# One decoder layer on one Trainium2 core: expert chunks, gathers and the last rows placed at other points of the program

## The chip, the cores and the metric

The kernel runs on one core of one Trainium2 chip. The metric is device time in microseconds (us) of one execution. The engines of the core are PE (TensorE: matmuls, with PEld its weight loads), DVE (VectorE), ACT (ScalarE), POOL (GpSimd) and SP (SyncE, used here only to issue DMAs). Each engine runs its instructions in the order in which they stand in its own stream; DMAs are issued by SP, ACT and POOL and move data on 16 shared DMA engines.

## The reference, cut to what matters

The layer has 512 tokens of width 1024. First comes a mixer; then, on the result x2, a retrieval layer (PEER) with 16384 experts:

```
x = x + merged @ W_out                       # attention and a gated recurrence, merged
h = rms_norm(x, norm_ffn_g)
q = (h @ w_q).reshape(B, S, 8, 2, 128)       # 8 heads, two half keys
sc = einsum('bshpd,phnd->bshpn', q, keys)    # 128 scores for each half key
v1, i1 = top_k(sc[..., 0, :], 16); v2, i2 = top_k(sc[..., 1, :], 16)
best, pos = top_k(v1 + v2 (all pairs), 16);  idx = i1 * 128 + i2 at pos
gates = softmax(best)
act = gelu(einsum('tkd,td->tk', u[idx], h))
x = x + einsum('tk,tkd->td', gates * act, v[idx])
return rms_norm(x, norm_final_g)
```

u and v have 16384 rows of 1024 float32 each. Every token uses 8 x 16 = 128 experts.

## The kernel before

Float32 operands of a matmul are split into a high part (`hi`, made on ACT at line 142) and a rest (`lo`, made on DVE at line 162, or 145), and three products are summed.

**Front** (lines 182 to 615): first RMS norm, projections, recurrence, attention, merge, x2, second norm. `tokens` (213 to 225) loads a piece of x transposed and scales it by `gm`, the first norm's scale vector, which line 275 loads through POOL's queue. `proj_tm` and `proj_fm` are the projections (lines 255 to 265).

**The expert layer is done in two ways.** Tokens 160 to 511 (DT = 352) are treated densely: expert row i2 = 0..127 is a *chunk* c. The U part of a chunk (`act_pieces`, line 638) loads 512 KB of u, splits it, makes 24 matmuls of 352 columns (line 646) and applies gelu; the result is a `gel` tile. The V part (lines 973 to 996) loads 512 KB of v, multiplies the gel tile with the chunk's gate weights G, and adds into six PSUM banks `acc` with 18 matmuls of 512 columns (lines 994 to 996). Tokens 0 to 159 (block 0 and 32 more) are treated by gathers: `gather` (704) has POOL fetch 128 rows of u or v by an indirect DMA into one of GB = 4 buffers, and `sparse` (711) uses them on DVE (line 715 for u, 725 for v). There are NS = 320 such steps: 160 for u, then 160 for v. `pace(goal, after)` (729) issues gathers up to a goal, and three gathers behind each one the DVE step, which is kept behind the instruction `after` on DVE.

**Routing** (lines 828 to 870): for 16 half keys hp a projection (24 matmuls of 512 columns), scores (line 847), top 16 of 128 on DVE (854 to 858), and per head the choice of 16 pairs (`route`, 752). `fill(n)` puts n whole U chunks between; here `int(F1*(hp+1)) - int(F1*hp)` per half key, which is 24 in all.

**G stage** (lines 876 to 917): after two more U chunks, the gates of the 352 tokens become dense matrices. For each 8 tokens DVE makes four one-hot tiles (904 to 907, two buffers `oh`), PE makes 8 small matmuls for each 4 tokens (912), ACT copies them out (914), and each 16 tokens are written to memory (`Gd`, 22 writes of 1 MB on ACT's queue). After each 4 tokens `piece` puts in a quarter of a U chunk, 88 quarters, so 22 chunks. Up to seven gathers are issued here.

**Transition** (938 to 945): three U chunks, loads of v, the load of the first G part (`g_load(0)`, which waits for the last write of Gd), gathers up to EARLY = 16, and two more U chunks, whose loads stand behind that of G on SP's queue.

**Loop** (973 to 1021) over the 128 chunks: V part of chunk c; until c = 115 the 75 U chunks that are left; `pace` by a share of the work done. **End** (1000 to 1029): at c = 120 x2 is loaded again; at c = 122 the 32 tokens' rows are finished; after the loop come the last gather steps, the rows of block 0 and those of `acc` (`final_rows`, 955: add, square, sum, scale, write).

KEEP = 53 gel tiles are live at once: 26 (LOOK) in a pool of their own, 17 (LATE) in `gel2`, which takes the memory that routing frees, and 10 in `extra`.

The order of each engine's stream is made by a planner with costs of its own from the order of the program; `tc.issue_after(x)` keeps an instruction behind x on x's engine, `keep_in_program_order` keeps it where it was written.

Of the kernel before, what the change touches and what calls it, by code (L numbers as in the profile page):

```python
# [6 lines left out]
F32 = mybir.dt.float32  # L7
# [5 lines left out]
OP = mybir.AluOpType  # L13
# [4 lines left out]
P = 128  # L18
# [8 lines left out]
NE = 128  # L27
# [4 lines left out]
DT = S - T0  # L32
# [14 lines left out]
VPRE = 2  # L47
GLAG = 3
GB = 4
TAILC = 2  # L50
HELD = 5
LASTU = 2
EARLY = 16
UEND = 116
TL = 2
F1 = 1.5


def host(inp):
# [57 lines left out]
def layer(nc, tc, a, out, probe=None, upto=99):  # L117
# [9 lines left out]
    def nm(s):  # L127
        uid[0] += 1
        return f"{s}_{uid[0]}"
# [25 lines left out]
    def wsplit(raw, shape, parts=1, eng=None):  # L155
        hi = oc.tile(list(shape), F32R, tag="hi", bufs=HB, name=nm("hi"))
        lo = oc.tile(list(shape), F32R, tag="lo", bufs=HB, name=nm("lo"))
        n = shape[1] // parts
        for i in range(parts):
            m = slice(i * n, (i + 1) * n)  # L160
            hi_of(hi[:, m], raw[:, m])
            (eng or V).tensor_tensor(lo[:, m], raw[:, m], hi[:, m].bitcast(F32), op=OP.subtract)  # L162
        return hi, lo


# [26 lines left out]
    with tc.tile_pool(name="front", bufs=1) as fr, tc.tile_pool(name="psf", bufs=1, space=PSUM) as psf:  # L192
# [79 lines left out]


        ktm, logf = [], []
        POOL.dma_start(gm, a["gmix"])
        POOL.dma_start(ones, a["const"][:, 5 * P:6 * P])
        ld = exp_ln_set()
        fb = proj_tm(0)
# [342 lines left out]
    with tc.tile_pool(name="peer", bufs=1) as pp, tc.tile_pool(name="psp", bufs=1, space=PSUM) as psp, ExitStack() as ps:  # L621
# [7 lines left out]
        def gel_tile(c):  # L629
            i = c % KEEP  # L630
            if i < LOOK:
                return pp.tile([P, DT], F32, tag="gel", bufs=LOOK, name=nm("gel"))
            if i < LOOK + LATE:
                return cur["gel2"].tile([P, DT], F32, tag="gel2", bufs=LATE, name=nm("gel"))
            return extra[i - LOOK - LATE]


        def act_pieces(c, pin=False):
# [33 lines left out]
        def piece(limit):  # L672
            while len(work) < 2 and nu[0] < limit:
                work.append(act_pieces(next(todo), True))
                next(work[-1])
                nu[0] += 1
            if work and next(work[0], 0) == 0:
                work.pop(0)
# [197 lines left out]
        with tc.tile_pool(name="gb", bufs=1, reuse_waits="tile") as gp:  # L876
            iT = gp.tile([P, 2, DT], F16, name="iT")
            gs = gp.tile([P, DT], F32, name="gs")
            g16 = gp.tile([P, 2, DT], F16, name="g16")
            fill(2)  # L880
            for n in range(1, NB):
                f = X if n == 1 else 0
                t = slice((n - 1) * P - X + f, n * P - X)
                b = bank((P, 4, P))
                for w in range(2):
                    PE.transpose(b[:, w, :], i12[:, w, n, :], ident)
                PE.transpose(b[:, 2, :], gta[:, n, :], ident)
                ACT.activation(iT[:, :, t], b[:, 0:2, f:], AF.Copy)
                ACT.activation(gs[:, t], b[:, 2, f:], AF.Copy, scale=GS)  # L889
                V.tensor_copy(g16[:, 0, t], gs[:, t])  # L890
                V.tensor_tensor(g16[:, 1, t], gs[:, t], g16[:, 0, t], op=OP.subtract)
            NQ = OT // QT
            shape = [P, NQ, P, QT]
            for s_ in range(NPT):
                G_ = gp.tile([P, NE, TG], F32, tag="G", bufs=2, name=nm("G"))
                for o in range(TG // OT):
                    t = slice(s_ * TG + o * OT, s_ * TG + (o + 1) * OT)

                    def row(x):
                        return x.rearrange("p (q t) -> p q t", t=QT).unsqueeze(2).to_broadcast(shape)  # L900

                    ioq = iok.unsqueeze(1).to_broadcast(shape)
                    oh = gp.tile([P, 3, NQ, P, QT], F16, tag="oh", bufs=2, name=nm("oh"))
                    V.tensor_tensor(oh[:, 0], ioq, row(iT[:, 0, t]), op=OP.is_equal)
                    V.tensor_tensor(oh[:, 2], ioq, row(iT[:, 1, t]), op=OP.is_equal)
                    V.tensor_tensor(oh[:, 1], oh[:, 2], row(g16[:, 0, t]), op=OP.mult)
                    last = V.tensor_tensor(oh[:, 2], oh[:, 2], row(g16[:, 1, t]), op=OP.mult)
                    for q in range(NQ):
                        b = bank((P, QT, P))
                        for i in range(QT):  # L910
                            for w in range(2):
                                lastg = tc.keep_in_program_order(PE.matmul(b[:, i, :], oh[:, 0, q, :, i], oh[:, 1 + w, q, :, i], start=w == 0, stop=w == 1))  # L912
                        m = o * OT + q * QT
                        ACT.activation(G_[:, :, m:m + QT].rearrange("p c t -> p t c"), b, AF.Copy)
                        piece(KEEP - HELD)
                ACT.dma_start(Gd.rearrange("g p s f -> s p g f")[s_], G_.rearrange("p (g c) t -> p g (c t)", c=GC))
                pace((s_ + 1) // 3, last.ins)
        late = ps.enter_context(tc.tile_pool(name="late", bufs=1, reuse_waits="tile"))
# [17 lines left out]
                return SP.dma_start(gts[g], Gd[g])  # L936

        with tc.issue_after(lastg.ins):
            fill(KEEP - nu[0] - LASTU)
        for c in range(VPRE):  # L940
            v_load(c)
        g0 = g_load(0)
        pace(EARLY, last.ins)
        with tc.issue_after(lastg.ins), tc.issue_after(g0.ins):
            fill(LASTU)

# [22 lines left out]

        todo_u = NE - nu[0]  # L970
        nu0 = nu[0]
        ready = []
        for c in range(NE):
            if c % GC == 0:
                g_load(c // GC + 1)
            gtile = gts[c // GC][:, :, (c % GC) * TG:(c % GC + 1) * TG]
            v_load(c + VPRE)
            vh, vl = wsplit(vraw.pop(c), [P, D])
            w = late.tile([P, DT], F32, tag="w", bufs=2, name=nm("w"))
            V.scalar_tensor_tensor(w.rearrange("p (s t) -> p s t", t=TG), gel.pop(c).rearrange("p (s t) -> p s t", t=TG),  # L980
                                   1.0 / GS, gtile, op0=OP.mult, op1=OP.mult)
            whi = late.tile([P, DT], F32R, tag="whi", bufs=2, name=nm("whi"))
            hi_of(whi, w)
            wlo = late.tile([P, DT], F32R, tag="wlo", bufs=2, name=nm("wlo"))
            last = V.tensor_tensor(wlo, w, whi.bitcast(F32), op=OP.subtract)  # L985
            ready.append((c, whi, wlo, vh, vl))
            if c < NE - TL or c == NE - 1:
                for tb in range(DB):
                    t = slice(tb * P, min(tb * P + P, DT))
                    m = t.stop - t.start  # L990
                    for i, whi, wlo, vh, vl in ready:
                        for hf in range(2):
                            d = slice(hf * 512, (hf + 1) * 512)
                            PE.matmul(acc[tb][hf][0:m, :], whi[:, t], vh[:, d], start=i == 0, stop=False)  # L994
                            PE.matmul(acc[tb][hf][0:m, :], whi[:, t], vl[:, d], start=False, stop=False)  # L995
                            PE.matmul(acc[tb][hf][0:m, :], wlo[:, t], vh[:, d], start=False, stop=i == NE - 1)  # L996
                ready = []
            fill(min(NE, nu0 + -(-todo_u * (c + 1) // UEND)) - nu[0])
            share = (c + 1 + nu[0] - nu0) / (NE - TAILC + todo_u)
            if c == NE - 8:  # L1000
                ld = exp_ln_set()
                yt = [e8([P, 2, D]) for _ in range(2)]
                ys = [yt[n // 2][:, n % 2, :] for n in range(NB)]
                gf = h20
                SP.dma_start(gf, a["gfin"].to_broadcast([P, D]))
                xf = xs_.rearrange("n p d -> (n p) d")
                yx = s4([P, D])
                SP.dma_start(yx[0:X, :], xf[P:T0])
                for n in range(NB):
                    t = T0 + (n - 1) * P if n else 0  # L1010
                    m = min(P, S - t)
                    SP.dma_start(ys[n][0:m, :], xf[t:t + m])
            if c == NE - 6:

                assert nsp[0] >= NS - sp0.w
                bs = []
                for hf in range(2):
                    bs.append(bank(tag="p"))
                    PE.matmul(bs[hf][0:X, :], fold[:, 0:X], sp1.ax[:, hf * 512:(hf + 1) * 512], start=True, stop=True)
                final_rows(yx[0:X, :], [b[0:X, :] for b in bs], P, X)  # L1020
            pace(EARLY + (NS - EARLY) * share, last.ins)

        while nsp[0] < NS:
            sparse(nsp[0])
            nsp[0] += 1
        final_rows(ys[0], [sp0.ax[:, 0:512], sp0.ax[:, 512:]], 0, P)
        for n in range(DB):
            m = min(P, DT - n * P)
            final_rows(ys[n + 1][0:m, :], [acc[n][hf][0:m, :] for hf in range(2)], T0 + n * P, m)
# [17 lines left out]
```

## Time and profile before

| | |
|---|---|
| Three runs | 1669.36, 1670.48, 1662.62 us; median 1669.36 |
| Profiled execution | 1675.46 us, its span 1673.7 us |
| Mean granted TensorE clock | 0.986 |
| PE busy | 1605.2 us (96%) |
| DVE busy | 1321.9 us (79%) |
| ACT busy | 709.6 us (42%) |
| POOL busy | 487.3 us (29%) |
| HBM traffic | 371.91 MB read, 27.39 MB written |

The profiled execution was the slowest of the four. Busy time of PE counts a matmul from its start to its modelled end; consecutive matmuls overlap, so 96% does not say that PE had no room. What PE can do is read from the spacing of matmuls that follow one another.

### The profile page before, as it was taken

The numbers are of one execution on the slowest core, as the hardware profiler recorded it, in microseconds if no ns is written. First come the engines' busy times: TensorE is split into PE (matmuls) and PEld (weight loads), VectorE is DVE, ScalarE is ACT, GpSimd is POOL, SyncE is SP. The second block draws the span as 40 slices with busy tenths as digits, with TensorE's granted clock in tenths as the row PEclk, the third lists the DMA queues.
The fourth block names the chain that finished last, engine by engine and source line by source line (L and its number), as shares of the span: only waits on it lengthen the run. The fifth ranks groups of instructions, "written<-read, shape, count | busy, mean of one in ns | idle before, by whom it ended". The sixth has DMA issues, their size and how long they took to land.

```text
span 1673.7 us, 23435 instructions
## 1 busy us (share of the span) xinstructions
PE 1605.2 (96%) x8511; PEld 1358.7 (81%) x8511; DVE 1321.9 (79%) x2560; ACT 709.6 (42%) x1152; POOL 487.3 (29%) x341
## 2 busy tenths in 40 slices
PE   8999999999999969997899999999999999999996
PEld 6877678888988869997788888887888888888874
DVE  8456663647999988887688888878888888888887
ACT  5433353234554547775333333333333333333333
POOL 4000000000000010002455555445455555554542
PEclk9999999999999979999899999999999999999998
DMA  5311133334333347888999999999999999999984
GB/s 173 101 51 51 51 104 111 103 115 154 108 109 116 103 126 192 219 224 265 336 340 353 349 368 349 337 341 339 344 368 351 359 354 347 360 358 363 343 305 145
DMA packets 197491, 400.87 MB, mean 240 GB/s; under 512 B 103344, under 2 KB 105904, under 8 KB 197376
## 3 DMA queue, kind: packets, MB, share of 16 engines
q1 hardware_dynamic: 58832, 206.02, 35.2%
q0 software_dynamic: 46336, 168.39, 27.0%
q10 hardware_dynamic: 92208, 24.98, 6.1%
q8 instruction: 66, 1.08, 0.3%
q14 instruction: 49, 0.40, 0.1%
HBM read 371.91 MB, written 27.39 MB: 239 GB/s over the span
## 4 chain that ended last, share of the span: by engine, by line
PE 53%; issue 16%; POOL 12%; DVE 12%; DMA 6%; ACT 1%; POOLq 0%; DVEq 0%; SPq 0%; ACTq 0%
PE b L646 13%; POOL ga L707 11%; PE b L263 5%; PE b L262 5%; PE b L995 5%; PE b L996 5%; PE b L265 4%; PE b L994 4%; DMA ga<-v,idx 4%; PE b L912 4%; DVE lo L162 3%; DMA ga<-un,idx 1%; DVE ti L858 1%; DVE mr L856 1%; DVE e L725 1%
## 5 line engine op out<-in xcount | busy, mean ns | idle before, releaser
L707 POOL DMA_INDIRECT ga<-un,idx x160 | 225.2, 1407 | 944.5 <-ACT gs L889 581.3
L646 PE MATMUL b<-hT,hi 128*128 128x352 f32 x2048 | 366.9, 327 | 2.2 <-ACT hi L142 1.7
L646 PEld LDWEIGHTS b<-hT,hi 128*128 128x128 f32 x2048 | 334.4, 190 | 12.7 <-ACT hi L142 2.0
L995 PE MATMUL b<-lo,whi 128*128 128x512 f32 (+1 forms) x768 | 305.0, 397 | 15.0 <-DVE lo L162 14.6
L996 PE MATMUL b<-hi,wlo 128*128 128x512 f32 (+1 forms) x768 | 304.3, 396 | 0.0
L994 PE MATMUL b<-hi,whi 128*128 128x512 f32 (+1 forms) x768 | 302.7, 395 | 0.0
L707 POOL DMA_INDIRECT ga<-v,idx x160 | 240.4, 1502 | 208.3 <-DVE e L725 190.3
L142 ACT ACTIVATE hi<-s 128x1024 fp32r<-128x1024 f32 (+1 forms) x195 | 205.1, 1052 | 203.1 <-PE b L646 88.1
L162 DVE TENSOR_TENSOR lo<-s,hi 128x1024 fp32r<-128x1024 f32 (+1 forms) x195 | 238.5, 1224 | 29.7 <-ACT hi L142 28.0
L142 ACT ACTIVATE whi<-w 128x352 fp32r<-128x352 f32 x128 | 63.7, 498 | 400.0 <-PE b L995 361.2
L725 DVE SCALAR_TENSOR_TENSOR e<-ga,wt,e 128x1024 f32<-128x1024 f32 x158 | 202.2, 1280 | 19.3 <-DMA ga<-v,idx 18.4
L715 DVE SCALAR_TENSOR_TENSOR ga<-ga,h 128x1024 f32<-128x1024 f32 x160 | 194.5, 1220 | 28.6 <-DMA ga<-un,idx 26.9
L646 PE MATMUL b<-hT,lo 128*128 128x352 f32 x1024 | 191.3, 325 | 11.8 <-DVE lo L162 11.8
L995 PEld LDWEIGHTS b<-lo,whi 128*128 128x128 f32 (+1 forms) x768 | 138.8, 181 | 59.2 <-DVE lo L162 22.0
L646 PEld LDWEIGHTS b<-hT,lo 128*128 128x128 f32 x1024 | 168.0, 189 | 12.4 <-DVE lo L162 12.3
L996 PEld LDWEIGHTS b<-hi,wlo 128*128 128x128 f32 (+1 forms) x768 | 138.5, 180 | 39.3
L994 PEld LDWEIGHTS b<-hi,whi 128*128 128x128 f32 (+1 forms) x768 | 138.2, 180 | 35.3 <-ACT hi L142 1.2
L142 ACT ACTIVATE hi<-vr 128x1024 fp32r<-128x1024 f32 x128 | 134.6, 1051 | 75.9 <-PE b L646 46.3
L162 DVE TENSOR_TENSOR lo<-vr,hi 128x1024 fp32r<-128x1024 f32 x128 | 156.1, 1220 | 9.4 <-ACT hi L142 9.4
L263 PE MATMUL b<-hT,hi 128*128 128x512 f32 (+1 forms) x376 | 146.4, 391 | 0.3 <-DVE hT L145 0.3
L262 PE MATMUL b<-hT,hi 128*128 128x512 f32 (+1 forms) x376 | 146.1, 390 | 0.2
L985 DVE TENSOR_TENSOR wlo<-w,whi 128x352 fp32r<-128x352 f32 x128 | 67.0, 523 | 80.9 <-ACT whi L142 77.5
(284 smaller groups left out, 1960.5 us busy)
## 6 DMA issues: line engine op xcount, KB each, us to landing
s<-uc SPq DMA_DIRECT2D x128, 512.0 KB
vr<-vc SPq DMA_DIRECT2D x128, 512.0 KB
Gd<-G ACTq DMA_DIRECT2D x22, 1024.0 KB
gt<-Gd SPq DMA_DIRECT2D x32, 704.0 KB
s<-wfm SPq DMA_DIRECT2D x30, 512.0 KB
s<-wq SPq DMA_DIRECT2D x16, 512.0 KB
s<-wmg SPq DMA_DIRECT2D x8, 512.0 KB
s<-wout SPq DMA_DIRECT2D x8, 512.0 KB
```

The lines of the kernel that those rows point to most:

```text
L142: ACT.activation(dst, src, AF.Copy)
L162: (eng or V).tensor_tensor(lo[:, m], raw[:, m], hi[:, m].bitcast(F32), op=OP.subtract)
L262: PE.matmul(b, wh[:, k, :], rh(i), start=start and i == 0, stop=False)
L263: PE.matmul(b, wh[:, k, :], rl(i), start=False, stop=False)
L646: m = PE.matmul(o, w[:, k, :], z[:, k, t], start=i == 0, stop=i == 3 * KD - 1)
L707: tc.keep_in_program_order(POOL.indirect_dma_start(out=t, out_offset=None, in_=a[src], in_offset=bass.IndirectOffsetOnAxis(ap=b.idx[:, j:j ...
L715: V.scalar_tensor_tensor(t, t, 1.0, h20, op0=OP.mult, op1=OP.mult, accum_out=b.act[:, j:j + 1])
L725: V.scalar_tensor_tensor(b.ax, t, b.wt[:, j:j + 1], b.ax, op0=OP.mult, op1=OP.add)
L985: last = V.tensor_tensor(wlo, w, whi.bitcast(F32), op=OP.subtract)
L994: PE.matmul(acc[tb][hf][0:m, :], whi[:, t], vh[:, d], start=i == 0, stop=False)
L995: PE.matmul(acc[tb][hf][0:m, :], whi[:, t], vl[:, d], start=False, stop=False)
L996: PE.matmul(acc[tb][hf][0:m, :], wlo[:, t], vh[:, d], start=False, stop=i == NE - 1)
```

## The change

Constants: F1 goes from 1.5 to 2.0 (32 U chunks in routing), TAILC from 2 to 8 (the divisor of `pace`'s share goes from 201 to 195), EARLY goes. The order of gel tiles is turned: `extra` before `gel2`. The U quarters that are left in the G stage (14 chunks, 56 quarters) are spread evenly over its 88 places. In the transition one gather follows each of three U chunks, so that ten have been issued when the loop begins. `gm` is loaded through ACT's queue. In the last group, that of chunks 126 and 127, the matmuls of one half of the row (both chunks) come before those of the other. The last gather steps and the final rows of block 0 move from behind the loop to chunk 123 in it.

```
-TAILC = 2
+TAILC = 8
-EARLY = 16
-F1 = 1.5
+F1 = 2.0
...
-        POOL.dma_start(gm, a["gmix"])
+        ACT.dma_start(gm, a["gmix"])
...
-            if i < LOOK + LATE:
-                return cur["gel2"].tile([P, DT], F32, tag="gel2", bufs=LATE, name=nm("gel"))
-            return extra[i - LOOK - LATE]
+            if i < LOOK + E8S:
+                return extra[i - LOOK]
+            return cur["gel2"].tile([P, DT], F32, tag="gel2", bufs=LATE, name=nm("gel"))
...
+            NPT_B = DT // QT
+            npc = 4 * (KEEP - HELD - nu[0])
...
-                        piece(KEEP - HELD)
+                        k = (s_ * TG + m) // QT
+                        if (k + 1) * npc // NPT_B > k * npc // NPT_B:
+                            piece(KEEP - HELD)
...
-            fill(KEEP - nu[0] - LASTU)
+            for _ in range(KEEP - nu[0] - LASTU):
+                fill(1)
+                pace(nga[0] + 1, cur["lo"].ins)
...
-        pace(EARLY, last.ins)
...
+        e0 = nga[0]
...
-                    for i, whi, wlo, vh, vl in ready:
-                        for hf in range(2):
-                            d = slice(hf * 512, (hf + 1) * 512)
+                    for hf in range(2):
+                        d = slice(hf * 512, (hf + 1) * 512)
+                        for i, whi, wlo, vh, vl in ready:
...
-            pace(EARLY + (NS - EARLY) * share, last.ins)
-
-        while nsp[0] < NS:
-            sparse(nsp[0])
-            nsp[0] += 1
-        final_rows(ys[0], [sp0.ax[:, 0:512], sp0.ax[:, 512:]], 0, P)
+            if c == NE - 5:
+                while nsp[0] < NS:
+                    sparse(nsp[0])
+                    nsp[0] += 1
+                final_rows(ys[0], [sp0.ax[:, 0:512], sp0.ax[:, 512:]], 0, P)
+            pace(e0 + (NS - e0) * share, last.ins)
```

`cur["lo"]` is the newest `lo` instruction of line 162, which `wsplit` now records.

## Rows read from the trace of the kernel before

**Rows 1.** Stage by stage: stretch, length, busy us (instructions) of each engine, clock, DMA share, GB/s.

```profile
390.00:596.00 206.00, 201.06 (x1118) 182.64 (x1117) 194.26 (x960) 109.06 (x236) 0.00 (x0) 1.00 0.35 115
596.00:613.00 17.00, 2.75 (x13) 2.30 (x14) 13.31 (x35) 7.47 (x27) 3.51 (x3) 0.60 0.30 95
613.00:786.00 173.00, 170.16 (x1230) 157.27 (x1228) 146.12 (x209) 121.04 (x131) 13.19 (x9) 0.99 0.78 213
786.00:819.00 33.00, 22.10 (x121) 21.52 (x121) 18.68 (x28) 8.80 (x13) 13.47 (x9) 0.84 0.96 335
819.00:1599.00 780.00, 769.18 (x3867) 656.36 (x3867) 662.04 (x851) 280.12 (x382) 409.03 (x291) 1.00 0.96 351
```

**Rows 2.** Longest pieces of the chain of waits: start, us, what.

```profile
289.54 1.81 PE b L265 x8
1081.57 3.80 PE b L646 x24
```

**Rows 3.** Timeline, end of routing and two steps of the G stage.

```profile
607.29 0.69 PE L886 MATMUL b<-ident,i 128*128 128x128 f32 x2 [11.42 <-DVE i L824]
...
765.71 0.82 PEld L912 LDWEIGHTS <-oh 128*128 128x128 f16 x8
...
767.63 0.82 PEld L912 LDWEIGHTS <-oh 128*128 128x128 f16 x8
```

**Rows 4.** Costliest groups, the page: busy, mean ns, idle before.

```profile
L162 DVE TENSOR_TENSOR lo<-s,hi 128x1024 fp32r<-128x1024 f32 (+1 forms) x195 | 238.5, 1224 | 29.7 <-ACT hi L142 28.0
```

**Rows 5.** DMA queues of the page: packets, MB, share of 16 engines over the span.

```profile
q1 hardware_dynamic: 58832, 206.02, 35.2%
q0 software_dynamic: 46336, 168.39, 27.0%
q10 hardware_dynamic: 92208, 24.98, 6.1%
```

**Rows 6.** Waits of SP's DMA queue: total us, times, longest.

```profile
SPq L936 <- DMA Gd<-G: 20.4, 1, 20.4
```

**Rows 7.** Timeline of the transition.

```profile
799.72 2.71 PE L646 MATMUL b<-hT,lo 128*128 128x352 f32 x8 [10.75 <-DVE lo L162]
...
818.82 0.40 PE L994 MATMUL b<-hi,whi 128*128 128x512 f32 x1
```

**Rows 8.** The loop, 819 to 1599 us: waits for gathers, and the costliest DVE group.

```profile
DVE ga L715 <- DMA ga<-un,idx: 17.3, 19, 2.4
DVE e L725 <- DMA ga<-v,idx: 13.9, 19, 1.6
...
L725 DVE SCALAR_TENSOR_TENSOR e<-ga,wt,e 128x1024 f32<-128x1024 f32 x141 | 180.5, 1280 | 14.8 <-DMA ga<-v,idx 13.9 <-DVE w L980 0.3
```

**Rows 9.** Three of the 40 equal stretches, columns as in Rows 1.

```profile
966.00:1008.00 42.00, 41.95 (x215) 35.92 (x214) 34.94 (x54) 15.95 (x22) 20.32 (x16) 1.00 0.99 368
1092.00:1134.00 42.00, 41.89 (x212) 35.55 (x211) 33.59 (x52) 14.99 (x21) 20.82 (x18) 1.00 0.95 333
1512.00:1554.00 42.00, 40.41 (x203) 33.99 (x202) 35.12 (x38) 14.66 (x20) 21.38 (x16) 1.00 0.99 361
```

**Rows 10.** Timeline of the end, and one piece of the chain there.

```profile
1653.36 1.28 DVE L725 SCALAR_TENSOR_TENSOR e<-ga,wt,e 128x1024 f32<-128x1024 f32 x1 [4.48 <-DMA ga<-v,idx]
1655.84 0.80 PE L995 MATMUL b<-lo,whi 128*128 128x512 f32 x1 [4.04 <-DVE lo L162]
1656.64 0.43 PE b L996
1663.06 2.73 DVE L967 SCALAR_TENSOR_TENSOR e<-e,rs,h 128x512 f32<-128x512 f32 x4
1665.78 0.68 DVE L960 TENSOR_TENSOR e<-e,b 96x512 f32<-96x512 f32 x1
```

**Rows 11.** The head: the first scaling's wait (timeline), the first weights' transfer (chain).

```profile
5.31 0.72 ACT L216 ACTIVATE hT<-s,gm 128x512 fp32r<-128x512 f32 x1 [3.29 <-DMA gm<-gmix]
1.66 4.17 DMA s<-wtm
```

More of the change, by code (lines that the diff above doesn't have):

```diff
@@ L161, in wsplit @@
             hi_of(hi[:, m], raw[:, m])
-            (eng or V).tensor_tensor(lo[:, m], raw[:, m], hi[:, m].bitcast(F32), op=OP.subtract)
+            cur["lo"] = (eng or V).tensor_tensor(lo[:, m], raw[:, m], hi[:, m].bitcast(F32), op=OP.subtract)
         return hi, lo
```

## The prediction

> **What bounds the kernel now.** I read the stage table first, because the page's shares mix stages with different limits. In [rows 1] PE is busy nearly throughout in routing, the G stage and the loop. Busy is not full, so I counted work by the spacing of matmuls: 24 of 352 columns take 3.80 us and eight of 512 columns 1.81 us, 0.226 each [rows 2]. A U chunk thus costs PE 3.80 us, a V part 18 x 0.23 = 4.1 us. The loop from 819 to 1599 us holds 75 U chunks and about 116 V parts: 75 x 3.8 + 116 x 4.1 = 761 of 780 us. PE bounds it, with the transfers right beside it: DMA share 0.96 at 351 GB/s. Routing from 390 to 596 us holds 26 U chunks (99 us), 15 projections of 24 matmuls (81 us) and 15 score groups of about 1.1 us (16 us), 196 of 206 us; DVE is busy 194 us of it. So PE is close to full almost everywhere, and moving PE work between stages pays only by the holes it closes. The holes are: 11.4 us at the end of routing, where PE waits for DVE's last index work [rows 3]; the transition, 33 us for five U chunks that need 19 [rows 1, 7]; the last chunk, where PE waits 4.0 us [rows 10].
>
> **The change part by part.** All terms are against the profiled execution, 1675.46 us (span 1673.7 and 1.8 around it), which lies 6.1 us above the median of 1669.36.
>
> *F1 = 2.0, routing.* Eight more U chunks: 8 x 3.80 = +30.4 us on PE. DVE gets 8 x 1.22 = 9.8 us more of `lo` [rows 4] and has room for it once each half key lasts 206/15 = 13.7 us plus 2. PE's small stalls may give back 1 us, and the hole at the end shrinks: with PE as the only bound DVE no longer trails the scores. Between closing none of the 11.4 us and all of it, I take 4. Sum +25, between +18 and +30.
>
> *G stage.* It loses those eight chunks. A step of four tokens lasts 767.63 - 765.71 = 1.92 us [rows 3], 0.82 of it for the eight small matmuls and 1.10 for the quarter chunk; 88 x 1.92 = 169 of the 173 us [rows 1], so PE set it. After: 88 x 0.82 + 56 x 1.10 = 134 us of PE. DVE now has 146 - 8 x 1.14 = 137 us (1.14 is the spacing of such instructions), so it becomes the bound, with PE just behind. DMA: 0.78 x 173 = 135 us, less eight loads of 1.5 us (q1 moves 206 MB in 0.352 x 1673.7 = 589 us, 350 GB/s, [rows 5]), 123 us: not the bound. Two `oh` buffers keep DVE and PE nearly in step, so two equal loads will not pack perfectly: I take 146 us, -27, between -36 (137) and -9 (164, half way back).
> Together: -2, between -18 and +21. The turned gel order only makes 32 chunks possible before routing's memory is free; `extra` holds nothing live then. I cost it at nothing; a wait for an old tenant would show as an ACT gelu wait.
>
> *Transition.* Now PE stands 10.75 us for a `lo` that is queued on DVE behind gather steps which wait for their data [rows 7]. After, each gather step stands behind its chunk's `lo`, so this wait goes. What is late next: the last two U chunks' loads stand on SP behind the load of G, and that one waits 20.4 us for the last write of Gd [rows 6], because up to nine gathers run beside it [rows 1]. Six gathers leave this stretch (sixteen to ten); one takes 0.270 x 1673.7 / 320 = 1.41 us of all DMA engines [rows 5], so the write can land up to 8.5 us sooner. Some of the six would have come after the write, so I take -7.5; the ends are 0 and -13.5 (33 us down to 19.5).
> The Trainium skill (DMA: Bandwidth & Descriptors, Queues, rings and completion order) says that each DMA engine takes turns between the queues that have work for it. By that, an estimate for the write among three busy queues is three times its own time (6.1% of 1673.7 us over about 23 MB of 25, some 4.5 us a write, [rows 5]), 13 us rather than the 20.4 us measured; by it fewer gathers in one queue would help less, 4 us instead of 7.5, and the sum would be 3.5 us worse. The trace's longer wait speaks for the larger value.
>
> *Loop.* The goal formula puts 285 gathers between the transition and c = 113 before, and 299 after (from 16 to 301, from 10 to 309): 14 more, 14 x 1.41 = 20 us of DMA in a stretch that has 0.04 x 780 = 31 us of it free. On DVE it is 14 x 1.28 = 18 us [rows 8] of 118 us free. So it can lie beside PE's work, but the DMA share becomes (749 + 20)/780 = 0.986. Stretches of 0.99 exist: one lost PE 0.05 us, another 1.6 of 42 [rows 9]. DVE waits for gathers only 38 times there, for some 285 of them [rows 8], so data mostly come in time now; that margin shrinks. The lower end is -3 (the loop starts with less in flight), the upper 21 (nothing hidden: 14 x 524 KB at 351 GB/s). I take +8, that is 0.4 us more in each of 18 such stretches.
>
> *End.* By the new divisor all gathers are issued at c = 119, not 125, and used at c = 123. So the 4.48 us wait of DVE for the last gather, with the last `lo` behind it, goes, and with it PE's 4.04 us [rows 10]. After that wait twelve matmuls ran 0.43 us apart instead of 0.23: 2.4 us. The final rows: the second half's add of the last rows began at 1665.78, held by four scalings of 2.73 us queued before it [rows 10], while the last matmul had ended at 1663.1: 2.7 us. With DVE free from 1650 us on and block 0's rows done at c = 123, this is gone too. -9. Block 0's six instructions now lie inside the loop, where DVE needs 2.3 us of each 4.1 us for the last V parts once gathers are over; they cost nothing there, 4 us if that cover failed. Turning the last group by halves lets the first half's add start 6 x 0.23 = 1.4 us sooner; it is off the path as the second half ends last: 0. Ends: -10 and -4.
>
> *gm on ACT's queue.* The first scaling waits 3.29 us for gm, until 5.31 us [rows 11]. But the first weights land at 1.66 + 4.17 = 5.83 us [rows 11], and PE needs their `hi` too: -0.2, between -3.3 (the whole wait) and 0. ACT is idle until then, so its issue costs nothing; POOL's `ones` load moves up.
>
> Sum: -2 - 7.5 + 8 - 9 - 0.2 = -10.7. Against its own time 1664.8 us; set on the median, 1669.4 - 10.7 = 1658.7, say 1659 us.
>
> **The rivals.**
> *The loop is already at the transfers' rate.* If 351 GB/s is what this mix can be given, nothing of the 14 gathers is hidden: loop +21, sum +2.3, 1672 us: no change. For it: share 0.96, and one stretch gave only 333 GB/s at share 0.95 [rows 9]. Against it: 368 GB/s in another, and DVE's few waits.
> The Trainium skill (DMA: Bandwidth & Descriptors, Specifications) puts HBM's limit per core at about 358 GB/s. By it, as an estimate, the loop's 351 x 0.780 = 274 MB and 7.3 more need 786 us, +6; that is close to my term and would leave the sum at -13. The trace does not hold that figure in every stretch (368).
>
> *The G stage does not shrink (the slower side).* If the 1.92 us step is set by the round from `oh` to PE to the freed buffer and not by the quarter chunks, taking 32 quarters away gives little: G stage 169, -4 instead of -27, while routing pays its +25. Sum -10.7 + 23 = +12, 1682 us. It decides from a G stage of 157 us upwards. For it: DVE and PE share two buffers. Against it: PE filled 170 of 173 us, while DVE had 27 us idle.
>
> *All holes close.* DVE and PE pack the G stage into 138 us (-35) and the loop hides its gathers (0): sum -10.7 - 8 - 8 = -27, 1643 us. For it: PE lost only 10.8 us in the loop. Against it: two engines at 98% in the G stage.
>
> **How the numbers follow.** A measurement can tell about 0.5% (8 us) from no change. Chances: my forecast 0.50 (its own range 1648 to 1669), the transfer rival 0.22, the slower rival 0.13, all holes 0.15. My forecast lies faster by over 0.5% in about 0.78 of its cases, within in 0.20, slower in 0.02; all holes always faster; the transfer rival 0.1, 0.65, 0.25; the slower one 0, 0.15, 0.85. That gives faster 0.39 + 0.15 + 0.02 = 0.56, same 0.10 + 0.14 + 0.02 = 0.26, slower 0.18. The range leaves out a part of the slower and of the all-holes case: 1641 to 1676.
>
> **What would show it.** The hole before line 886 near 625 to 633 us and shorter than 11 us; the G stage's step near 1.66 us and its end about 2 us sooner than now; SP's wait for Gd near 12 us and the first V matmul some 9 us sooner than at 818.8; in the loop more waits of DVE for gathers and a DMA share of 0.98; no wait of DVE for a gather after c = 123, matmuls 0.23 us apart to the end, and about 8 us from the last of them to the end of the span. I am wrong if the G stage lasts over 157 us, if the loop from the first V matmul to the last U matmul (818.8 to 1599 now) grows by more than 15 us, or if the last V group still waits.

## The result, and the profile after

The changed kernel takes 1676.99 us (median of 9 runs, 1673.39 to 1679.31), the kernel before 1664.87 us (9 runs) beside it: ratio 1.0055, interval [1.0033, 1.0077]. It is slower, by some 9 us by the ratio (12 by these two medians); forecast were 1659 us, in a range from 1641 to 1676, and a gain. The time lies between the transfer rival's 1672 and the slower rival's 1682, but neither gives the reason: the experiments refute the first, and the G stage, which by the second was not to shrink, did (149 us for 173).

The first views are the stages after, to be read against [rows 1].

```profile
600.00:631.00 31.00, 21.10 (x122) 20.02 (x121) 27.09 (x108) 15.29 (x38) 2.37 (x2) 0.89 0.30 95
631.00:780.00 149.00, 141.19 (x1040) 130.26 (x1039) 130.93 (x194) 97.28 (x109) 6.65 (x7) 0.98 0.80 214
780.00:811.00 31.00, 21.30 (x120) 21.01 (x121) 17.40 (x26) 13.60 (x18) 10.12 (x7) 0.83 0.87 287
811.00:1612.00 801.00, 774.27 (x3873) 656.79 (x3871) 680.70 (x872) 279.85 (x383) 425.25 (x306) 1.00 0.96 351
1612.00:1677.00 65.00, 56.51 (x239) 41.86 (x237) 47.84 (x67) 26.21 (x54) 8.20 (x5) 0.96 0.50 177
```

Up to the loop all is a little early: the first V matmul starts at 811.0 us for 818.8. The loop then takes 801 us for 780. GB/s and DMA share in it are those of before, so its 15 more gathers (302 for 287, 8 MB on 274) took longer in proportion: this looks like the rival by which the transfers' rate is full.

The waits inside that loop (who waits for what, total us, times, longest), to be read against [rows 8]:

```profile
DVE ga L714 <- DMA ga<-un,idx: 31.4, 30, 2.8
PE b L1000 <- DVE lo L161: 26.5, 23, 3.2
...
DVE e L724 <- DMA ga<-v,idx: 22.6, 33, 1.8
```

DVE's waits for gathers rose from 31 us in 38 cases to 54 us in 63. DVE runs in order, so V parts' `lo` stand behind such a wait, and PE behind them: 26.5 us here, 10.5 us before, by this row of the first profile of the kernel before:

```profile
PE b L995 <- DVE lo L162: 10.5, 12, 3.2
```

Four more places, from the head, routing's end, the transition and the end of the changed kernel. First the timeline, answering [rows 11, 3]; then SP's waits for Gd, answering [rows 6] (line 932 loads v, line 939 loads G); then the chain at the end, answering [rows 10]:

```profile
3.76 0.72 ACT L215 ACTIVATE hT<-s,gm 128x512 fp32r<-128x512 f32 x1 [1.29 <-DMA gm<-gmix]
...
5.54 0.79 PE L254 MATMUL b<-hi,hT 128*128 128x512 f32 x1 [5.54 <-ACT hi L141]
...
626.86 0.69 PE L885 MATMUL b<-ident,i 128*128 128x128 f32 x2 [7.94 <-DVE i L823]
```

```profile
SPq L932 <- DMA Gd<-G: 11.8, 1, 11.8
...
SPq L939 <- DMA Gd<-G: 7.2, 1, 7.2
```

```profile
1663.06 0.23 PE b L999
1663.29 0.23 PE b L1000
1663.52 0.24 PE b L1001
1663.76 0.02 issue
1663.78 0.70 DVE e L964
```

The first scaling waits 2 us less for gm, and the hole at routing's end is 3.5 us smaller. SP's wait at the load of G fell from 20.4 to 7.2 us, but most of the difference only moved: a load of v just ahead of it now waits 11.8 us for a write of Gd, so SP waits 19.0 us in all. At the end matmuls run 0.23 us apart to the last, and DVE takes up the first final row 0.02 us behind it.

### The profile page after: what moved, and what is told of

It reads as the page before. It is cut to its first block, busy times and chain, and to the rows that moved or that the text cites. A ratio compares the mean times of both kernels' runs of the same rounds, so it can differ in the third digit from the quotient of the medians.

```text
span 1677.2 us, 23441 instructions
## 1 busy us (share of the span) xinstructions
PE 1605.0 (96%) x8511; PEld 1359.9 (81%) x8511; DVE 1326.6 (79%) x2560; ACT 699.5 (42%) x1152; POOL 471.1 (28%) x340
## 4 chain that ended last, share of the span: by engine, by line
PE 55%; DMA 17%; issue 10%; POOL 8%; DVE 7%; ACT 2%; DVEq 0%; POOLq 0%; ACTq 0%; SPq 0%
PE b L645 14%; DMA ga<-v,idx 8%; POOL ga L706 8%; DMA Gd<-G 7%; PE b L262 6%; PE b L264 6%; PE b L261 6%; PE b L1000 5%; PE b L1001 5%; PE b L999 5%; DVE lo L161 2%; ACT G L915 1%; PE b L846 1%; PE b L913 1%; DVE e L724 1%
## 5 line engine op out<-in xcount | busy, mean ns | idle before, releaser
L706 POOL DMA_INDIRECT ga<-un,idx x160 | 220.4, 1378 | 955.9 <-ACT gs L888 603.8
L645 PE MATMUL b<-hT,hi 128*128 128x352 f32 x2048 | 364.1, 327 | 10.7 <-ACT hi L141 10.2
L706 POOL DMA_INDIRECT ga<-v,idx x160 | 230.1, 1438 | 193.4 <-DVE e L724 172.7
L990 DVE TENSOR_TENSOR wlo<-w,whi 128x352 fp32r<-128x352 f32 x128 | 66.8, 522 | 62.3 <-ACT whi L141 60.0
```

Of the source, the lines that this page charges most:

```text
L645: m = PE.matmul(o, w[:, k, :], z[:, k, t], start=i == 0, stop=i == 3 * KD - 1)
L706: tc.keep_in_program_order(POOL.indirect_dma_start(out=t, out_offset=None, in_=a[src], in_offset=bass.IndirectOffsetOnAxis(ap=b.idx[:, j:j ...
```

## The experiments

"Loop" is the time from the first V matmul to the start of the last U matmul, "end" from there to the span's end, all from one profile of each kernel. A ratio is to the kernel before, run beside it. Medians of different groups of runs compare less well than ratios: the kernel before had medians from 1664.87 to 1668.01 us beside them.

| run | U placed | gather buffers | first V | loop | end | median us | ratio |
|---|---|---|---|---|---|---|---|
| before, first profile | old | 4 | 818.8 | 780.6 | 74.3 | 1664.87 | |
| e1 before again | old | 4 | 819.8 | 779.5 | 68.3 | 1667.97 | 1.0015 [0.9999, 1.0030] |
| changed | new | 4 | 811.0 | 800.7 | 65.5 | 1676.99 | 1.0055 [1.0033, 1.0077] |
| e9 changed again | new | 4 | 815.5 | 787.9 | 65.0 | 1674.73 | 1.0052 [1.0028, 1.0076] |
| e2 14 fewer gathers | new | 4 | 814.9 | 777.7 | 65.6 | 1656.57 | 0.9946 [0.9929, 0.9963] |
| e3 half V loads | new | 4 | 808.9 | 782.8 | 64.9 | 1661.62 | 0.9965 [0.9947, 0.9983] |
| e4 old divisor | new | 4 | 814.6 | 790.0 | 66.3 | 1668.52 | 1.0016 [0.9996, 1.0037] |
| e8 old U | old | 4 | 808.2 | 792.5 | 65.7 | 1667.44 | 0.9998 [0.9979, 1.0018] |
| e13 old U, old divisor | old | 4 | 808.9 | 785.7 | 67.1 | 1663.47 | 0.9987 [0.9972, 1.0002] |
| e10 before, new U | new | 4 | 822.2 | 773.4 | 67.6 | 1671.12 | 1.0025 [1.0004, 1.0046] |
| e11 three buffers | new | 3 | 816.5 | 890.3 | 66.8 | 1771.43 | 1.0627 [1.0583, 1.0670] |
| e5 five buffers | new | 5 | 816.9 | 768.9 | 64.9 | 1652.42 | 0.9909 [0.9882, 0.9936] |
| e6 before, five | old | 5 | 821.3 | 765.6 | 67.9 | 1654.40 | 0.9923 [0.9894, 0.9953] |
| e7 five, old divisor | new | 5 | 817.0 | 766.5 | 67.2 | 1653.37 | 0.9907 [0.9873, 0.9941] |
| e12 five, old U | old | 5 | 814.1 | 769.4 | 65.7 | 1647.12 | 0.9879 [0.9855, 0.9903] |
| e15 five, even spread | F1 1.5 | 5 | 813.8 | 767.7 | 65.1 | 1649.64 | 0.9896 [0.9869, 0.9924] |
| e14 five, half moved | F1 1.75 | 5 | 806.3 | 768.1 | 64.9 | 1642.68 | 0.9867 [0.9836, 0.9897] |

**Is it the program or the execution? e1 and e9**, each an unchanged kernel.

> The kernel before, unchanged, for a second profile of it. Its first profiled execution (1675.5 us) lay 10.6 us above the median of nine runs (1664.9). If that surplus sits in one place, this profile shows where: with a time near 1665 us I expect the first V matmul at 818 to 819 us as before, and the 10 us missing in the loop (780 us from the first V matmul to the last U matmul, so 770) or in the wait for the last gather (4 us). If the profile adds its surplus everywhere, no stage differs by more than 3 us.

> The changed kernel a second time, unchanged, for a second profile of it. If the loop of 800.7 us (first V matmul to last U matmul) belongs to the program, it comes again within 3 us, with a time near 1677; if it belonged to that one execution, as 6 us of the end did in the first profile of the kernel before, the loop is nearer 792 and the undone U placement explains nothing.

The 4.48 us wait of DVE for the last gather in [rows 10] did not come again: in e1 the wait for the last `lo` is 0.44 us, and the end 68.3 us for 74.3 (67.6 in e10, which has the same end).

```profile
1652.21 0.19 PEld L995 LDWEIGHTS b<-lo,whi 128*128 128x128 f32 x1 [0.44 <-DVE lo L162]
```

Nor did the loop of 801 us come again: e9's profile has 788, with DVE's waits for gathers at 37 us in 46 cases and PE's for `lo` at 15.8 us. That is not within the 3 us asked for, yet the median did come again. So a loop from one profile of this kernel is good to some 6 us each way, and smaller differences are read from medians below.

**Gathers or bytes? e2, e3 and e4.**

> The changed kernel with the last 14 of the 320 gather steps left out (the last 14 experts of block 0), so that the loop issues about 285 gathers up to chunk 113, as the kernel before does, and all else stays. Theory 'rate' (the loop is at the transfers' rate, and each added gather of 512 KB lengthens it by its own transfer): the loop, 802 us in the changed kernel, falls by 13 to 14 times 1.45, about 19 us, to 783; the time by about as much. Theory 'order' (gathers are issued late and awaited in DVE's order, whatever their number): 13 of 299 fewer waits, the loop falls by 1 to 4 us.

```
-  [(sp0, "v", j) for j in range(sp0.w)]
+  [(sp0, "v", j) for j in range(sp0.w - 14)]
```

> The changed kernel, but each V load brings only the first half of the row, which is used twice (the output is another one); the instructions on PE, DVE, ACT and POOL, and the gathers, are the same in number and size. It takes 256 KB of some 2400 KB per chunk from the DMA engines. Theory 'rate': the waits for gathers nearly go, the loop falls from 802 us to PE's own 761 to 772 us, DMA share 0.9 or less. Theory 'order': the waits of DVE for gathers (63 of them, 54 us, in the changed kernel) stay within a third, and the loop stays above 790 us.

```
-  vraw[c] = late.tile([P, D], F32, tag="vr", ...);  SP.dma_start(vraw[c], a["vc"][c])
+  vraw[c] = late.tile([P, D // 2], F32, tag="vr", ...);  SP.dma_start(vraw[c], a["vc"][c][:, 0:D // 2])
   (hi and lo still made over the full row, from the half read twice)
```

> The changed kernel with the divisor of the gathers' share back at 201 (TAILC 2), and the last gather steps and block 0's rows again behind the loop; the transition and the U chunks stay changed. About 290 gathers up to chunk 113 instead of 299. Theory 'rate': the loop falls by 9 times 1.45 = 13 us to 789, the end (64 us from the last U matmul on) grows by 8 to 10 us as the last gather is late again; total 3 to 5 us less than the changed kernel. Theory 'order': the loop stays within 4 us of 802 and the total is 5 to 10 us more.

```
-TAILC = 8
+TAILC = 2
-            if c == NE - 5: (the rest of the gathers' use and block 0's rows)
+        (the same, after the loop)
```

The loop's windows of e2 and e3, columns as in [rows 1]:

```profile
815.00:1593.00 778.00, 768.64 (x3873) 655.98 (x3872) 663.58 (x859) 280.71 (x383) 410.91 (x291) 1.00 0.95 351
```

```profile
809.00:1592.00 783.00, 770.01 (x3872) 657.84 (x3871) 678.92 (x875) 280.83 (x382) 443.73 (x306) 1.00 0.91 321
```

Taking away 14 gathers (7 MB) gives the loop back whole; by the ratios (0.9946 for 1.0055) it is worth 18 us. Taking away 30 MB of V loads, four times the bytes, gives no more: it runs at only 321 GB/s and is still 783 us long, between what the two theories said for it. If bytes at a fixed rate set the time, e3 would have ended far ahead of e2. So what counts is the gathers themselves. Other traffic counts too, but less by the byte, and the packets show by what: in e3 a gather's last one comes 6.1 us after its issue, for 6.5 in the changed kernel, and DVE's waits for gathers are 27 us for 54. The old divisor alone gives 6 to 8 us of median back; its end is 66.3 us for 65.5, where 8 to 10 us more were expected.

**The ring of buffers: e5, e6, e7 and e11.** A gather can be issued only when DVE has used the one that was in the same buffer, so it has one round of the ring, buffers times period, to be written, to land and to be used. That theory asks for another number of buffers.

> The changed kernel with five gather buffers instead of four (room made by one scratch tile taken from the load buffers and one index tile moved to the routing memory; the order in which DVE uses the gathers stays). Theory 'ring': a buffer's round (POOL's issue, 6.5 us in the first third until the last packet is in, some 2 us until DVE can start, 1.3 us of DVE, 0.3 us back to POOL) is about 10 us, so four buffers give a gather every 2.5 us at best, and the changed loop wants one every 2.55; a fifth allows one every 2.0 us. Then the loop falls from 801 us to 770 to 780 and the time by 20 to 30 us. Theory 'rate' (bytes per second are the limit): a fifth buffer adds no bandwidth, the loop stays within 5 us of 801.

> The kernel before with five gather buffers, made in the same way. Theory 'ring': the kernel before wants a gather every 2.67 us and is just inside what four buffers give; its loop (780 us, of which PE's own work is 761) falls by 5 to 10 us. The transition gets worse or stays: the early gathers are still queued ahead of the chunks' rest on DVE. Total 5 to 10 us less than before. Theory 'rate': no change within 4 us.

> The changed kernel with five buffers and the divisor at 201 with block 0's rows behind the loop. Theory 'ring': with the ring wide enough the number of gathers in the loop no longer counts, so the loop is within 4 us of the five-buffer kernel's with divisor 195, and this one is slower by what its end costs, 1 to 8 us. Theory 'rate': the loop is about 10 us shorter than that kernel's, as with four buffers (790 against 801).

> The changed kernel with three gather buffers for four, the use of a gather two (for three) behind its issue. By the theory that the round of a gather buffer, 10 us, sets the loop, a gather can be had every 10 / 3 = 3.3 us, and some 280 in the loop make it 280 x 3.3 = 930 us or more, time about 1810. By the theory of the byte rate the same bytes pass at the same rate: loop 800 to 815, time about 1680 to 1690.

```
-GB = 4          e5, e6, e7: GB = 5        e11: GB = 3, GLAG = 2
+GB = 5          (two small tiles moved to other memory, to make room for it)
```

The same waits, with five buffers (e5) and with three (e11), and the two loops' windows:

```profile
PE b L1000 <- DVE lo L161: 2.9, 4, 1.3
...
DVE ga L713 <- DMA ga<-un,idx: 2.7, 3, 1.2
...
DVE e L723 <- DMA ga<-v,idx: 1.7, 3, 1.1
```

```profile
817.00:1586.00 769.00, 765.78 (x3872) 655.85 (x3871) 673.20 (x868) 280.73 (x382) 446.30 (x304) 1.00 0.97 365
```

```profile
DVE ga L714 <- DMA ga<-un,idx: 81.7, 73, 3.2
PE b L1000 <- DVE lo L161: 81.3, 44, 5.3
DVE e L724 <- DMA ga<-v,idx: 73.4, 68, 3.9
```

```profile
817.00:1707.00 890.00, 802.23 (x3870) 672.18 (x3870) 686.02 (x872) 280.54 (x382) 427.77 (x304) 0.97 0.88 314
```

With five buffers the changed kernel loses almost nothing to gathers: the same bytes pass in 769 us at 365 GB/s, and PE is busy 766 of them. That refutes the rate rival: 351 GB/s was what the ring asked for, not what the memory could give. With three buffers the same bytes take 890 us. (The two tiles that make room belong to routing and the G stage, ahead of the loop; moving them alone was not tried.) Put together, from the number of gathers issued in each loop:

| kernel | gathers in the loop | loop / gathers | one round | DVE's waits for gathers |
|---|---|---|---|---|
| e11, three | 300 | 2.97 us | 8.9 us | 155 us, 141 times |
| changed, four | 302 | 2.65 | 10.6 | 54 us, 63 times |
| e1 before, four | 285 | 2.73 | 10.9 | 30 us, 38 times |
| e5, five | 300 | 2.56 | 12.8 | 4.4 us |

PE's own work of 766 us would have a gather every 766/285 = 2.69 us before and every 766/302 = 2.54 us after, a round of 10.1 us with four buffers. In the changed kernel a gather's last packet on POOL's queue comes 6.5 us after its issue (mean of the 90 from the 20th on). Where DVE waited for its gather it began 1.5 us later still, 8.6 us behind the issue (57 cases); then 1.3 us of use and 0.3 us until POOL issues again: 10.2 us. Before, there was just enough room, on the mean; the change takes 0.6 us of it, and each gather that comes later than the mean is a wait.

One prediction from this held: with five buffers the divisor costs nothing (e5 and e7 are level). The kernel before gains from a fifth buffer too, but 13 us (e6, 0.8%) where 5 to 10 were expected: it was already losing time to its ring. And three buffers were to give 930 us or more and gave 890. The round isn't a constant: with three buffers an issue waits 3.4 us for its first packet, with four 3.8 and with five 4.1, and where DVE waited, with three, it began 7.2 us behind the issue, which makes a round of 8.8 us, near the 8.9 of the table. The ring is shown as the limit; its 10 us are only a size for four buffers.

**The moved U chunks: e8, e10, e12.**

> The changed kernel with the U chunks placed as before (F1 1.5, a quarter after each four tokens, old order of the gel tiles); transition, gathers, end as changed. Both theories: the loop stays about 801 us, as it has the same gathers. Before it: routing ends near 606 us and the G stage near 781 again, so the first V matmul comes at 811 to 813, level with the changed kernel, if the transition's new order is what gained there; at 816 or later if the moved U chunks gained it.

> The kernel before with the placement of U alone: F1 2.0, the quarters spread evenly, the order of the buffers for the U chunks; the pacing of the gathers, the transition, the end and the order of the V matmuls stay as before. If moving the U chunks costs 8 us in the loop by itself, the loop is 788 +- 3 and the time some 1673 to 1678. The theory of the four gather buffers, by which what counts in the loop is how often a gather is asked for, sees no change in that here: loop 780 +- 3, time 1662 to 1668.

> The changed kernel with a fifth gather buffer and the placement of U as before, so that the rest of the change (transition, pace of the gathers, end) stands alone beside five buffers. If the moved U chunks cost time only where the ring of buffers is short, it comes out at the 1652 of five buffers with the moved chunks, loop 769; if they cost it by something else, at 1652 - 9 = 1643, loop 761.

```
-F1 = 2.0
+F1 = 1.5
-   k = (s_ * TG + m) // QT
-   if (k + 1) * npc // NPT_B > k * npc // NPT_B:
-       piece(KEEP - HELD)
+   piece(KEEP - HELD)          (and gel_tile's old order; e10: the reverse, on the kernel before)
```

The new placement costs 7 to 10 us in the changed kernel (e8), 4 us of median alone on the kernel before (e10), 5 us with five buffers (e12 to e5). e10 came out between its two expectations (1671 us, for up to 1668 or from 1673 on), and so did e12 (1647 for 1652 or 1643). After e8 I held that most of this lay in the loop. e9 and e10 say otherwise: their loops of 788 and 773 us are no longer than without it. What all pairs share is a later first V matmul: 811.0 and 815.5 for 808.2; 822.2 for 819.8; 816.9 for 814.1. Steadier still is the issue of the first load of G, which waits for the last write of Gd: 795.4 and 796.0 us for 789.7 (e8), 805.9 for 800.3 (e10 and e1), 799.3 for 792.8 (e5 and e12), some 6 us later in each pair. The DMA pieces of the changed kernel's chain of waits near the G stage's end (start, us, what) show why:

```profile
735.37 6.52 DMA Gd<-G
741.99 6.89 DMA Gd<-G
748.99 9.10 DMA Gd<-G
758.19 8.52 DMA Gd<-G
771.63 9.68 DMA Gd<-G
785.01 10.33 DMA Gd<-G
```

The emptied G stage runs from write to write of its slices: two `G` buffers, and ScalarE's copies wait for the write of the slice before the last (39.5 us of waits in that stage; with the old placement and five buffers, none). So the stage stops shrinking, and what stands behind those copies on ScalarE is late. That accounts for some 6 us; whether the rest of e8's 7 to 10 lies there too was not shown. The timeline of the transition, in the changed kernel and then in e8:

```profile
781.39 1.02 ACT L915 ACTIVATE G<-b 128x512 f32<-128x512 f32 x1 [5.64 <-DMA Gd<-G]
...
787.05 3.30 PE L645 MATMUL b<-hT,hi 128*128 128x352 f32 x10 [7.58 <-ACT hi L141]
```

```profile
782.87 2.81 PE L645 MATMUL b<-hT,hi 128*128 128x352 f32 x16 [1.71 <-ACT hi L141]
```

SP's waits for Gd in e8, 10.3 us in all where the changed kernel has 19.0:

```profile
SPq L937 <- DMA Gd<-G: 8.8, 1, 8.8
...
SPq L930 <- DMA Gd<-G: 1.5, 1, 1.5
```

**Where the last two parts lie: e13, e14, e15.**

> The changed kernel with both the placement of U and the pace of the gathers in the loop as before (the divisor with a tail of 2, the last tokens' sums after the loop); what is left of the change is the transition's gathers, the order of the V matmuls and the scale vector's queue. If the rate at which the gathers are asked for is what lengthens the loop when there are four buffers, its loop is 780 to 784 for the 792 of the undone placement alone, and the time 1658 to 1662 for 1667. If the loop's length there has another cause (the transition's gathers running ahead), it stays at 1667 with a loop of 790.

> The changed kernel with five gather buffers and F1 1.75, so that half as many U chunks leave the G stage for the routing as in the change. If the placement costs 5 us because the G stage, emptied of its U quarters, waits for its own writes at its end (and ScalarE with it), half of it leaves that stage bound by its matmuls: G ends near 781, the hole ahead of the transition's first chunk is 2 to 6 us for 11, and the time is at or below the 1647 of the old placement with five buffers. If each chunk that is moved costs its share, the time is 1649 to 1650.

```
e14: five buffers, F1 = 1.75          e15: five buffers, F1 = 1.5          e13: e8's edit and e4's
```

> The changed kernel with five gather buffers and F1 1.5, so that no chunk is moved, while the even spread of the quarters over the G stage and the new order of the buffers for the U chunks stay. If the 5 us hang on the moved chunks, it gives the 1647 of the old placement with five buffers; if they hang on the spread or on the order, the 1652 of the new one.

e13 against e8 gives 4 us back where 5 to 9 were expected; its loop is 786, not 780 to 784. So with the old placement of U the pace of the gathers explains 4 us (with the new one, e4, 6 to 8 us), and the rest of that loop's extra length stays although the divisor is the old one. In e13 the loop starts 11 us sooner than in e1 but ends only 4.7 us sooner (1594.6 for 1599.3), which fits gathers that can't be had sooner; that this is the cause was not tested further.

e14 moves half of the chunks and is the fastest of all: 1642.68 us, 1.3% below the kernel before. Its G stage's start, the transition's hole and the two stages (columns as in [rows 1]):

```profile
610.83 0.69 PE L885 MATMUL b<-ident,i 128*128 128x128 f32 x2 [7.72 <-DVE i L823]
780.10 4.38 PE L645 MATMUL b<-hT,hi 128*128 128x352 f32 x16 [1.73 <-ACT hi L141]
```

```profile
615.00:778.00 163.00, 156.99 (x1135) 145.09 (x1135) 138.28 (x199) 112.12 (x123) 10.90 (x9) 0.96 0.92 231
778.00:806.00 28.00, 22.66 (x122) 22.09 (x121) 19.15 (x29) 10.48 (x15) 11.56 (x8) 0.88 0.96 329
```

Half the move makes routing end 7.7 us later than in e12 (610.8 for 603.1) and the G stage 12 us shorter (162 for 174), with a hole of only 1.7 us at its end; the whole move makes it end 21 us later (e5, 624.5), while the stage stops at its writes. e15, with nothing moved, lies between e12 and e5, so the even spread and the buffers' order may cost 2 us or nothing. The intervals of the five-buffer kernels overlap (3 rounds each); that e14 is ahead of e12 rests on the medians (4 us; 2 by the ratios) and on its first V matmul, 8 us sooner.

## Why the prediction was wrong, point by point

- **Routing and G stage** (-2): right in sum, not in reason. The last small matmul of the G stage starts at 778.2 and 778.8 us in the two profiles, 2 us sooner than in e1 (780.5): the transposes start 22 us later than there (626.9 for 604.7, forecast 25), and the stage behind them is 24 us shorter (forecast 27). The hole before the transposes is 7.94 us, at 626.9, and the stage 149 us for a forecast 146. The bound is not DVE but the writes of Gd: from 660 us on the chain of waits goes from one write to the next, and the prediction had counted them only as traffic. The slower rival (no shrinking) did not come.
- **Transition** (-7.5): about -4.5 (32.8 and 36.7 us from that matmul to the first V matmul, 39.3 in e1). The 10.75 us wait for `lo` [rows 7] is gone, as said; but PE then stood 7.58 us for ScalarE's `hi`, and SP's waits for Gd fell only from 20.4 us [rows 6] to 19.0. With the old placement of U (e8) the same transition brings them to 10.3 us and the first V matmul to 808.2, 11.6 us sooner than in e1: the step was sound by itself, and the moved U chunks took back much of it. The prediction costed the two parts apart, and asked what is late next on SP and not on ScalarE. First V matmul: 811.0 and 815.5, forecast some 810.
- **Loop** (+8): the failed step. It was +21 in the first profile and +8 in the second. The mean of the two, 15, lies within the range given, and by the sign that the prediction set itself (15 us more) only the first profile shows it wrong. But e2 prices the 14 gathers alone at 18 us, near the end of the range that meant "nothing hidden". The DMA share stayed at 0.96, where 0.98 was forecast. The step put a gather at 1.41 us of DMA and 1.28 us of DVE, both with room, and took DVE's 38 short waits as a sign of margin. They were the sign that the ring of four buffers was already at its limit. The cost belongs to the time between issue and use, which neither busy share shows. e2, e5 and e11 show this.
- **End** (-9): -3. The end is 65 us, as forecast, but the kernel before ends in 68.3 us in e1. This term is the second that failed: 6 us of its gain were read from waits that did not come again, in an execution slower than all nine runs beside the changed kernel: 1675.46 us, 10.6 above their median.
- **gm**: the first matmul starts at 5.54 us for 6.61 (5.27 for 6.43 in the second profiles); -1.1 for -0.2.
- **The transfer rival** (+21, 1672) had the time almost right and the reason wrong. The Trainium skill (DMA: Bandwidth & Descriptors, Specifications) puts HBM's limit at about 358 GB/s for a core. The trace of e5 differs, with 365 GB/s over 769 us.

With e1 as the base and the mean of the two profiles after, it adds up to: before the loop -6.5, loop +14.8, end -3.1, so +5; the medians, which carry e1's 1.4 us above and those profiles' 1 us below, say about +8, beside the ratio's 9. Forecast was -10.7: of the 19 us between, some 7 are the loop's, 6 the end's, 3 that of the part before the loop, and 2 to 3 the executions'.

## What to carry to other kernels

When a stream of gathers goes through a ring of buffers, compare one round of the ring (buffers times the period at which gathers are wanted) with the time from issue to use; busy shares of DMA and of the engine don't show this limit, and a bound that looks like bandwidth should be tried with one more buffer. Work moved out of a stage pays only until the next bound of that stage, here the write of its output: move half and look. And before a wait of a few microseconds is entered as a gain, see it in a second execution.

## What was not expected of the hardware

- The write of one slice of Gd (22 of them, 1 MB each) took 6.5 to 10.3 us in the chain above, and 14.2 us once in e5, where the prediction had estimated 4.5 us of the engines' time.
- A gather's first packet comes 3.4 to 4.1 us after POOL's issue, the more the more buffers the changed kernel has, and its packets then take 2.6 us.
- The same program's loop differs by 13 us between two executions (801 and 788) whose times differ by 9. With five buffers the loops of all six kernels profiled lie between 765.6 and 769.4.
